# The low halves of seven weight factors: adding DMAs in place of VectorE subtractions

## The chip, the cores and the metric

The kernel runs on one core of a Trainium2 chip. Its time is the device time of one execution in microseconds. Before the change it is 1282.74 us, the median of three runs between 1281.86 and 1282.98.

## What is computed

Two decoder layers over 512 tokens of width 1024, in float32. Each layer projects `x` into three parallel mixers (pooling, retention, sparse attention), projects their concatenation back, adds and normalises, and then runs a gated feed-forward network (FFN) of 2816 columns:

```python
hg = x @ w_gate
hp = jnp.pad(hg, ((0, 0), (CONV_WIDTH - 1, 0), (0, 0)))
hc = conv_b
for kk in range(CONV_WIDTH):
    hc = hc + hp[:, kk:kk + t] * conv_w[kk]
return (jax.nn.gelu(hc) * (x @ w_up)) @ w_down
```

## The kernel before, in words

**Halves.** TensorE works on float32r, a rounded float32. Each float32 operand is therefore split into a high half (the value rounded to float32r) and a low half (what the rounding left), and each product is three matmuls: high by high, high by low, low by high.

**The FFN.** The 2816 columns are 22 groups `f` of 128. In each layer groups 0 to 2 are computed plainly (`ff_plain`). Groups 3 to 21 take gate and up projections together by a scheme of seven block products (`ff_seven`), whose weight operands are called 11, t1, 21, t2, 22, t3 and t4. Each is a tile `w` of 128x2x4x128 numbers (high half and low half, 128x512 each) and is used by one product: 12 matmuls of 256 columns. Between these products stand the matmuls of the down projection (`mm<-w,hT`, 512 columns).

**How a group's weights come about** (`load_seven`). Four DMAs of 256 KB on SyncE's queue fill two tiles `raw`, called b and r here as in the code. VectorE makes two more raw tiles from them by additions: t13 (one addition of 128x1024) and t24 (two of 128x512). From the slices of these four tiles the seven operands are split (`split`): ScalarE writes the high half, and a subtraction writes the low half, on the engine that the table `SEVEN` names (v VectorE, p GpSimd). Groups 20 and 21 of a layer always use VectorE. There are 5 buffers for raw tiles (`NR`) and 14 for w tiles (`NW`); the down projection's weights go through the same buffers, with their low halves by GpSimd (`LO_FFN`). A raw tile's buffer comes free when its last reader is done.

**The order.** All operations are recorded first. A planner (`Plan.schedule`) then gives each engine a fixed order, from a price for each operation (`price`), the latencies between engines, and the number of free buffers; on the chip each engine keeps that order and waits on semaphores. `shares` tells the planner which operations of VectorE and GpSimd it must not place beside each other. A semaphore wait in an engine's or a queue's order holds all that is behind it.

```python
b, r = raw_tile(2, 4, P), raw_tile(2, 4, P)
for out, src in ((b[:, 0], wg[:, 0]), (r[:, 0], wu[:, 0]), (b[:, 1], wu[:, 1]), (r[:, 1], wg[:, 1])):
    nc.sync.dma_start(out, src)
```

Of the kernel before, what the change touches and what calls it, by code (L numbers as in the profile page):

```python
# [10 lines left out]
AF = mybir.ActivationFunctionType  # L11
OP = mybir.AluOpType
AX = mybir.AxisListType
F = mybir.dt.float32
# [11 lines left out]
NFF = FF // P  # L26
# [126 lines left out]
class Plan:  # L153
# [49 lines left out]
    def shares(self, e, m, seen):  # L203

        if e == "vector":
            source = [v for read, v in seen if read and not v.tile.psum and int(np.prod(v.shape[1:])) > 1]
            return len(source) > 1 or (m in ("tensor_scalar", "tensor_copy") and not any(v.tile.psum for _, v in seen))
        return e == "gpsimd" and m != "memset"

    def price(self, op, seen):  # L210
        def size(v):
            return int(np.prod(v.shape[1:]))

        n = max([size(v) for _, v in seen] or [1])
        e, m = op.engine, op.method
        if e == "tensor":
            if m == "transpose":
                return 56 if op.args[2].shape[1] == 64 else 110
            n = size(op.args[2])
            return max(107, n * 0.4537)  # L220
        if e == "scalar":
            extra = sum(isinstance(op.kwargs.get(k), View) for k in ("bias", "scale")) + ("accum_out" in op.kwargs)
            return n * 0.833 + (52 if any(v.tile.psum for _, v in seen) else 95) + 92 * extra
        if e == "vector":
            if m == "reciprocal":
                return 6.3 * n + 70
            scalars = sum(isinstance(a, View) for a in (op.args[2:4] if m == "tensor_scalar" else op.args[2:3]))
            if m in ("tensor_scalar", "tensor_copy") and not any(v.tile.psum for _, v in seen):
                return 0.52 * n + 70 + 58 * scalars
            return 1.04 * n + 70 + 55 * scalars * (m == "scalar_tensor_tensor")  # L230
        if e == "gpsimd":
            if m == "memset":
                return n * 0.9 + 20
            if m == "tensor_copy":
                return n * 3.33 + 120
            if m == "tensor_scalar":
                return n * 1.24 + 120
            if op.args[-1] == OP.pow:
                return n * 165 + 300
            return n * 2.16 + 120  # L240
        byte = n * 4 * max(v.shape[0] for _, v in seen)
        return byte / 330.0

    def schedule(self):
# [35 lines left out]
        def opened(op):  # L280

            out = []
            for t in op.tiles:
                if t.got is None:
                    out.append(t)
                    if t.psum:
                        out += [f for f in t.follow if f.got is None and f not in out]
            return out
# [43 lines left out]
        while left:  # L332
            best = None
            for e in self.ENGINES:
                now = free[e]
                w, r = waiting[e], ready[e]
                while w and w[0][0] <= now:
                    heapq.heappush(r, heapq.heappop(w)[1:])
                cand = None
                skipped = []  # L340
                while r:
                    i = heapq.heappop(r)
                    skipped.append(i)
                    at = placed_at(ops[i[1]])
                    if at is not None and at <= now:
                        cand = (now, *i)
                        break
                    if len(skipped) > LOOK:
                        break
                if cand is None:  # L350

                    opts = []
                    for i in skipped:
                        at = placed_at(ops[i[1]])
                        if at is not None:
                            opts.append((at, *i))
                    for t0, *i in heapq.nsmallest(LOOK, w):
                        at = placed_at(ops[i[1]])
                        if at is not None:
                            opts.append((max(at, t0), *i))  # L360
                    if opts:
                        cand = min(opts)
                for i in skipped:
                    heapq.heappush(r, i)
                if cand is not None and (best is None or cand < best[:3]):
                    best = (*cand, e)
            assert best is not None, "no place for any instruction that is ready"
            start, _, i, e = best
            op = ops[i]
            if (op.rank, i) in ready[e]:  # L370
                ready[e].remove((op.rank, i))
                heapq.heapify(ready[e])
            else:
                waiting[e] = [x for x in waiting[e] if x[2] != i]
                heapq.heapify(waiting[e])
            op.start = start
            end = start + op.cost
            if e == "scalar" and op.method == "activation":
                f = op.args[2]
                if any(f in s for s in FUNCTIONS) and f not in functions:  # L380
                    functions = next(s for s in FUNCTIONS if f in s)
                    end += 1290
            if op.shared:
                held[e == "vector"] = end
            free[e] = end
            if e == "sync":
                free[e] = start + 60
                dma = max(getattr(self, "dma", 0.0), start + 600)
                self.dma = dma + op.cost
                end = self.dma + 1500  # L390
            elif e == "gpsimd":
                free[e] = end + 100
            op.opens = opened(op)
            op.wait = -1
            for t in op.opens:
                place = min(slots[t.key])
                slots[t.key].remove(place)
                t.got, t.after = place[0], place[2]
                if t.psum:
                    used[t.psum] += 1  # L400
            for t in op.tiles:
                t.last, t.by = max(t.last, end), e
                t.left -= 1
                if t.left == 0:
                    slots[t.key].append((t.last + 200, next(number), t))
                    if t.psum:
                        used[t.psum] -= 1
            for u in op.users:
                u.wait -= 1
                u.ready = max(u.ready, end + LATENCY[e][u.engine] * SLACK["wait"])  # L410
                if u.wait == 0:
                    heapq.heappush(waiting[u.engine], (u.ready, u.rank, u.index))
            done.append(op)
            left -= 1
# [12 lines left out]
def trunk(tc, x_d, pos_d, w_in, w_out, w_gate, w_up, w_down, cst_d, prm_d,  # L427
          w1k_d, w1v_d, w2k_d, w2v_d, poolw_d, gn_d, ln1g_d, ln1b_d, ln2g_d, ln2b_d, out_d):
    nc = Plan(tc.nc)
    from contextlib import ExitStack  # L430
    es = ExitStack()
    with es:
# [36 lines left out]
        def engine(who):  # L469
            return nc.gpsimd if who == "p" else nc.vector  # L470
# [46 lines left out]
        def load_seven(l, f):  # L517

            wg, wu = (w[l].rearrange("(h k p) c -> p h k c", p=P, h=2)[:, :, :, f * P:(f + 1) * P] for w in (w_gate, w_up))
# [3 lines that stand above are left out]
            t13, t24 = raw_tile(2, 4, P), raw_tile(2, 4, P)  # L523
            out = {}

            def split(name, src):
                w = w_tile(2, 4, P)
                nc.scalar.copy(w[:, 0], src)
                engine("v" if f >= NFF - 2 else SEVEN[name]).tensor_tensor(w[:, 1], src, w[:, 0].bitcast(F), OP.subtract)
                out[name] = (w[:, 0], w[:, 1])  # L530

            split("11", b[:, 0])
            nc.vector.tensor_tensor(t13, b, r[:, 0:1].to_broadcast([P, 2, 4, P]), OP.add)
            split("t1", t13[:, 0])
            split("21", r[:, 1])
            nc.vector.tensor_tensor(t24[:, 0], t13[:, 0], b[:, 1], OP.add)
            split("t2", t24[:, 0])
            split("22", b[:, 1])
            nc.vector.tensor_tensor(t24[:, 1], t24[:, 0], r[:, 1], OP.add)
            split("t3", t13[:, 1])  # L540
            split("t4", t24[:, 1])
            return out
# [1060 lines left out]

LO_MIX, LO_FFN = "pvv", "p"

SEVEN = {"11": "v", "21": "p", "22": "v", "t1": "v", "t2": "v", "t3": "v", "t4": "v"}

WHO = "vpvp"

# [63 lines left out]
```

## Time and profile before

| what | value |
|---|---|
| median of three runs | 1282.74 us |
| profiled execution, its own time | 1283.03 us |
| span in its profile | 1281.2 us |
| TensorE (PE) busy | 1259.2 us (98%) |
| VectorE (DVE) busy | 1041.5 us (81%) |
| ScalarE (ACT) busy | 707.7 us (55%) |
| GpSimd (POOL) busy | 342.1 us (27%) |
| DMA, mean rate over the span | 96 GB/s |

The span runs from the first to the last instruction; 1.83 us of the profiled execution's own time lie outside it. Busy times are sums of an engine's instructions. A matmul's end is modelled, so the rate of TensorE is read from how many matmuls end in a stretch, not from its busy time. PEld is the loading of weights into TensorE, SPq SyncE's DMA queue.

### The profile page before, as it was taken

How to read it: one execution, taken by the hardware profiler on the slowest of the kernel's cores; microseconds unless marked ns; L12 is line 12 of the kernel's file. 1: busy time of each engine (PE TensorE's matmuls, PEld its weight loads, DVE VectorE, ACT ScalarE, POOL GpSimd, SP SyncE). 2: the span in 40 equal slices, each digit the busy share in tenths (PEclk: the TensorE clock that was granted, in tenths of full speed). 3: DMA queues.
4: the chain of work that ended last, by engine and by line, in shares of the span. 5: the costliest groups of instructions: out<-in, count | busy, mean ns of one | idle time of the engine just before them, and what ended most of it. 6: DMA issues, size and time to landing. Idle time of an engine off the chain costs nothing.

```text
span 1281.2 us, 21536 instructions
## 1 busy us (share of the span) xinstructions
PE 1259.2 (98%) x8044; PEld 1124.9 (88%) x8044; DVE 1041.5 (81%) x1957; ACT 707.7 (55%) x1459; POOL 342.1 (27%) x256
## 2 busy tenths in 40 slices
PE   8999999999999999999999999999999999999996
PEld 6889898879999999999888988888899999999995
DVE  7857896888888988888785788869887989888876
ACT  5445575775655555555333464767565555555540
POOL 1141321424322322212112331233323222222023
PEclk9999999999999999999999999999999999999998
DMA  8422252101343433345342233320023333334321
GB/s 271 120 66 81 87 183 62 34 1 50 93 113 91 128 91 107 109 128 155 121 141 75 67 91 115 124 69 16 2 88 94 92 98 108 117 101 130 98 68 67
DMA packets 142601, 123.24 MB, mean 96 GB/s; under 512 B 6688, under 2 KB 116000, under 8 KB 142496
## 3 DMA queue, kind: packets, MB, share of 16 engines
q1 hardware_dynamic: 142496, 121.86, 31.5%
q8 instruction: 63, 1.03, 0.3%
q14 instruction: 42, 0.34, 0.1%
HBM read 117.65 MB, written 4.19 MB: 95 GB/s over the span
## 4 chain that ended last, share of the span: by engine, by line
PE 93%; DVE 2%; ACT 2%; issue 1%; POOL 1%; DMA 0%; SPq 0%; POOLq 0%; ACTq 0%
PE mm L424 46%; PE s L424 38%; PE tr L424 5%; PE pv L424 4%; ACT P L424 1%; DVE sm L424 1%; DMA x<-in_x 0%; POOL w L424 0%; DVE ps L424 0%; DVE CTl L424 0%; POOL y L424 0%; ACT ot L424 0%; ACT y L424 0%; ACT w L424 0%; DVE w L424 0%
## 5 line engine op out<-in xcount | busy, mean ns | idle before, releaser
L424 POOL TENSOR_TENSOR w<-raw,w 128x1024 fp32r<-128x1024 f32 (+3 forms) x116 | 234.2, 2020 | 663.2 <-ACT w L424 375.0
L424 ACT CAST w<-raw 128x512 fp32r<-128x512 f32 (+2 forms) x403 | 290.9, 742 | 189.1 <-PE s L424 117.8
L424 DVE TENSOR_TENSOR w<-raw,w 128x512 fp32r<-128x512 f32 (+3 forms) x288 | 234.2, 833 | 41.9 <-ACT w L424 36.0
L424 PE MATMUL mm<-w,hT 128*128 128x512 f32 (+1 forms) x1074 | 264.1, 391 | 1.1 <-POOL w L424 1.1
L424 PE MATMUL s<-xq,w 128*128 128x256 f32 x1944 | 250.0, 281 | 0.7 <-ACT xq L424 0.7
L424 PEld LDWEIGHTS s<-xq,w 128*128 128x128 f32 x1944 | 242.6, 189 | 7.1 <-ACT xq L424 1.2
L424 PE MATMUL mm<-w,xT 128*128 128x512 f32 (+3 forms) x1152 | 238.7, 355 | 1.8 <-DVE w L424 1.8
L424 PE MATMUL s<-xs,w 128*128 128x256 f32 x1824 | 234.3, 281 | 0.0
L424 PEld LDWEIGHTS s<-xs,w 128*128 128x128 f32 x1824 | 226.3, 189 | 2.6
L424 PEld LDWEIGHTS mm<-w,hT 128*128 128x128 f32 x1074 | 193.1, 188 | 38.5 <-POOL w L424 1.7
L424 PEld LDWEIGHTS mm<-w,xT 128*128 128x128 f32 x1152 | 191.0, 189 | 26.6 <-ACT xT L424 2.0
L424 DVE TENSOR_TENSOR raw<-raw,raw 128x512 f32<-128x512 f32 (+1 forms) x114 | 106.7, 936 | 5.8 <-DMA raw<-in_w_up 4.3
L424 DVE TENSOR_TENSOR y<-y,mm 128x512 f32<-128x512 f32 (+1 forms) x97 | 63.3, 675 | 22.7 <-PE mm L424 22.3
L424 ACT COPY pq<-s 128x256 f32<-128x256 f32 x152 | 55.3, 368 | 45.5 <-PE s L424 44.9
L424 PE MATMUL mm<-w,mixT 128*128 128x512 f32 x240 | 74.9, 425 | 0.0
L424 POOL TENSOR_TENSOR sm<-sm,mhalf 128x1 f32<-128x1 f32 (+1 forms) x28 | 27.3, 974 | 158.9 <-DVE sm L424 152.2
L424 DVE SCALAR_TENSOR_TENSOR pq<-gu,prm,pq 128x511 f32<-128x511 f32 x76 | 65.8, 865 | 3.1 <-ACT pq L424 2.9
L424 DVE TENSOR_TENSOR PT<-tr,PT 128x384 fp32r<-128x384 f32 (+1 forms) x96 | 49.2, 540 | 9.9 <-ACT PT L424 9.2
L424 ACT ACTIVATE P<-s,sm 128x128 f32<-128x128 f32 (+3 forms) x96 | 49.5, 526 | 13.4 <-DVE sm L424 13.1
L424 ACT CAST PT<-tr 128x384 fp32r<-128x384 f32 (+1 forms) x96 | 41.4, 473 | 23.5 <-PE tr L424 23.1
L424 PEld LDWEIGHTS mm<-w,mixT 128*128 128x128 f32 x240 | 42.2, 189 | 9.9 <-issue 0.2
L424 PE MATMUL mm<-xT,w 128*128 128x512 f32 x192 | 49.6, 400 | 0.0
(195 smaller groups left out, 1676.4 us busy)
## 6 DMA issues: line engine op xcount, KB each, us to landing
raw<-in_w_gate SPq DMA_DIRECT2D x76, 256.0 KB, 3.6
raw<-in_w_up SPq DMA_DIRECT2D x76, 256.0 KB, 4.1
raw<-in_w_down SPq DMA_DIRECT2D x36, 512.0 KB, 4.1
raw<-in_w_in SPq DMA_DIRECT2D x32, 512.0 KB, 4.3
raw<-in_w_out SPq DMA_DIRECT2D x14, 512.0 KB, 3.7
raw<-in_w_in SPq DMA_DIRECT2D x8, 530.0 KB, 4.2
raw<-in_w_down SPq DMA_DIRECT2D x16, 256.0 KB, 2.8
raw<-in_w_in SPq DMA_DIRECT2D x8, 384.0 KB, 3.2
```

Source lines behind the costliest of these rows:

```text
L424: getattr(getattr(self.nc, op.engine), op.method)(*a, **k)
```

## The change

In `split`, the letter d now stands for a third way: ScalarE writes the low half's place with the negative of the value, rounded as the high half is (a copy with scale -1.0), and a DMA issued by GpSimd adds the value to it (`accum_op=OP.add`, from the raw tile to the w tile, 256 KB). All seven operands are set to d, so in groups 3 to 19 of both layers the subtractions are gone. The planner prices the issue at 900 ns on GpSimd, puts the end 4500 ns behind it, and does not count it as sharing with VectorE. The scratch space for GpSimd's DMA descriptors grows from 1024 to 4096 bytes a partition.

```diff
-        return e == "gpsimd" and m != "memset"
+        return e == "gpsimd" and m not in ("memset", "dma_start")
...
         if e == "gpsimd":
+            if m == "dma_start":
+                return 900
...
                 free[e] = end + 100
+                if op.method == "dma_start":
+                    end += 4500
...
                 nc.scalar.copy(w[:, 0], src)
-                engine("v" if f >= NFF - 2 else SEVEN[name]).tensor_tensor(w[:, 1], src, w[:, 0].bitcast(F), OP.subtract)
+                who = "v" if f >= NFF - 2 else SEVEN[name]
+                if who == "d":
+
+                    nc.scalar.activation(w[:, 1], src, AF.Copy, scale=-1.0)
+                    nc.gpsimd.dma_start(w[:, 1], src, accum_op=OP.add)
+                else:
+                    engine(who).tensor_tensor(w[:, 1], src, w[:, 0].bitcast(F), OP.subtract)
...
-SEVEN = {"11": "v", "21": "p", "22": "v", "t1": "v", "t2": "v", "t3": "v", "t4": "v"}
+SEVEN = {"11": "d", "21": "d", "22": "d", "t1": "d", "t2": "d", "t3": "d", "t4": "d"}
...
-    nc = bacc.Bacc("TRN2", target_bir_lowering=False, num_devices=1, dynamic_dma_scratch_size=1024)
+    nc = bacc.Bacc("TRN2", target_bir_lowering=False, num_devices=1, dynamic_dma_scratch_size=4096)
```

## Rows read from the trace of the kernel before

**Rows 1.** The page, part 1: busy time, share of the span, instructions.

```profile
PE 1259.2 (98%) x8044; PEld 1124.9 (88%) x8044; DVE 1041.5 (81%) x1957; ACT 707.7 (55%) x1459; POOL 342.1 (27%) x256
```

**Rows 2.** Stretches of layer one's FFN: length; PE, PEld, DVE, ACT, POOL busy; clock, DMA, GB/s.

```profile
452.99:529.71 76.72, 76.72 (x539) 71.61 (x539) 65.80 (x96) 43.69 (x83) 19.50 (x12) 1.00 0.34 100
529.71:585.92 56.21, 56.21 (x416) 53.34 (x416) 48.88 (x75) 32.85 (x66) 8.76 (x6) 1.00 0.40 120
```

**Rows 3.** Waits of PE, 288 to 660 us: total, times, longest.

```profile
PE mm L424 <- DVE sm L424: 0.6, 1, 0.6
PE mm L424 <- POOL w L424: 0.5, 1, 0.5
```

**Rows 4.** Chain that ended last: start, us, what; two of six like it.

```profile
452.99 7.08 PE s L424 x60
...
529.71 7.07 PE s L424 x60
```

**Rows 5.** ACT by shape, 452.99 to 529.71: busy, mean ns; idle before.

```profile
L424 ACT CAST w<-raw 128x512 fp32r<-128x512 f32 x40 | 24.2, 621 | 23.7 <-PE s L424 19.7 <-PE mm L424 2.2 <-DVE raw L424 0.8
...
L424 ACT ACTIVATE gu<-pq 128x512 f32<-128x512 f32 x5 | 3.2, 632 | 4.3 <-DVE pq L424 4.3
```

**Rows 6.** POOL by shape, 452.99 to 529.71.

```profile
L424 POOL TENSOR_TENSOR w<-raw,w 128x512 fp32r<-128x512 f32 x9 | 12.7, 1411 | 42.4 <-DVE raw L424 14.0 <-PE s L424 12.2 <-PE mm L424 8.9
L424 POOL TENSOR_TENSOR w<-raw,w 128x1024 fp32r<-128x1024 f32 x3 | 7.6, 2548 | 19.4 <-PE s L424 19.4
```

**Rows 7.** Groups by shape, whole span: low halves of 128x512.

```profile
L424 DVE TENSOR_TENSOR w<-raw,w 128x512 fp32r<-128x512 f32 x234 | 166.8, 737 | 27.6 <-ACT w L424 25.4
...
L424 POOL TENSOR_TENSOR w<-raw,w 128x512 fp32r<-128x512 f32 x52 | 74.3, 1429 | 260.4 <-ACT w L424 136.1 <-DVE raw L424 41.5 <-PE mm L424 38.3
```

**Rows 8.** Timeline of SyncE's queue, one group's loads and the next's: start, us.

```profile
472.00 0.37 SPq L424 DMA_DIRECT2D raw<-in_w_gate  x1
472.41 1.05 SPq L424 DMA_DIRECT2D raw<-in_w_up  x2
...
484.14 2.05 SPq L424 DMA_DIRECT2D raw<-in_w_down  x2
487.61 0.37 SPq L424 DMA_DIRECT2D raw<-in_w_gate  x1
```

**Rows 9.** Timeline of DVE, the same group's additions and subtractions.

```profile
478.87 1.21 DVE L424 TENSOR_TENSOR raw<-raw,raw 128x1024 f32<-128x1024 f32 x1
...
480.34 0.68 DVE L424 TENSOR_TENSOR raw<-raw,raw 128x512 f32<-128x512 f32 x1
...
483.91 3.67 DVE L424 TENSOR_TENSOR w<-raw,w 128x512 fp32r<-128x512 f32 x4
488.23 0.69 DVE L424 TENSOR_TENSOR w<-raw,w 128x512 fp32r<-128x512 f32 x1 [0.65 <-ACT w L424]
...
489.61 0.69 DVE L424 TENSOR_TENSOR w<-raw,w 128x512 fp32r<-128x512 f32 x1
```

**Rows 10.** DMA, 452.99 to 529.71: queue's share; issues, KB, us to landing.

```profile
q1 hardware_dynamic: 11808, 7.60, 33.6%
...
raw<-in_w_gate SPq DMA_DIRECT2D x10, 256.0 KB, 3.4
raw<-in_w_up SPq DMA_DIRECT2D x10, 256.0 KB, 4.2
raw<-in_w_down SPq DMA_DIRECT2D x3, 512.0 KB, 4.1
```

**Rows 11.** DMA, whole span: quickest and slowest large ones.

```profile
lnb<-in_ln1b SPq DMA_DIRECT2D x2, 512.0 KB, 6.9
...
out_x<-y SPq DMA_DIRECT2D x2, 256.0 KB, 2.1
```

**Rows 12.** Timeline of DVE, low half of t1 of group 19.

```profile
560.60 0.69 DVE L424 TENSOR_TENSOR w<-raw,w 128x512 fp32r<-128x512 f32 x1
```

**Rows 13.** Timeline of PE, first product with it.

```profile
567.47 1.09 PE L424 MATMUL s<-xs,w 128*128 128x256 f32 x8
```

## The prediction

> **What bounds the kernel now.** I read the page's busy times first: TensorE is busy 98% of 1281.2 us, VectorE 81%, ScalarE 55%, GpSimd 27% [rows 1]. Since a busy TensorE is not one at its peak, I then read stretches of the FFN: over 76.72 us in the middle, five groups of columns, and over 56.21 us near its end TensorE has no idle time at all, at the full clock [rows 2]. Third, TensorE's own waits in the FFN of layer one are 0.6 and 0.5 us, one each [rows 3]; layer two gives the same two figures. Fourth, the chain of waits: bursts of 60 matmuls of 256 columns, 7.08 us each or 118 ns a matmul, come back once a group, six of them from 452.99 to 529.71, so a group takes 76.72/5 = 15.34 us, and TensorE's rate is the same in each [rows 4]. The reader is to see that VectorE, at 86% here (65.80 of 76.72, rows 2), holds TensorE up almost nowhere. What relieving it can give back in both FFNs is 2 x (0.6 + 0.5) = 2.2 us, 0.17%. A measurement of this kernel can tell about 0.2% (2.6 us) from no change. So the question is what the new way costs.
>
> **What goes, and what comes.** Groups 3 to 19 of two layers are 34 groups of seven operands, 238 splits. Gone are 6 x 34 = 204 VectorE subtractions of 0.737 us, 150 us, and 34 on GpSimd of 1.43 us, 49 us [rows 7]. None stands on TensorE's path beyond the 2.2 us above, so I count their going at nothing. Come 238 negations on ScalarE; the nearest rows are the high half itself, 0.621 us, and another function on 128x512, 0.632 us [rows 5]. That is 238 x 0.63 = 150 us. In the five-group stretch it is 35 x 0.63 = 22.1 us on top of 43.69, so ScalarE goes to 65.8 of 76.72, 86%. It is the new busiest engine after TensorE, but it fits. Come also 238 DMA issues on GpSimd, which no row shows. Below, SyncE's issues take about 0.4 us [rows 8]; above, GpSimd's subtraction of the same operand takes 1.43 us. I take 1 us, between the two. In the stretch GpSimd loses five subtractions (7.1 us) of its 19.50 and gains 35 us: 47 of 76.7, 62%. GpSimd is in order, so an issue waits behind a down subtraction of 2.55 us [rows 6] or an earlier issue whose negation is late, and the next down subtraction waits behind it.
>
> **The wait that is longer.** Before, a low half follows its high half by one subtraction. Now it follows by a second ScalarE pass, an issue and a landing. Call L the time from the negation's end to the landing. The trace has no adding DMA and none from buffer to buffer. From below: 256 KB out to memory land in 2.1 us; from above: the slowest large load lands in 6.9 us [rows 11]. The nearest are loads of the same 256 KB, 3.4 and 4.2 us from issue to landing [rows 10]. I take L = 5.0: 4.2, and 0.8 for GpSimd's slower issue and its queue.
>
> The Trainium skill (DMA: Bandwidth & Descriptors, section "Anatomy of one DMA — SWDGE (gpsimd) path") fits a DMA of GpSimd by 2.0 us plus bytes at 436 GB/s, an estimate of 2.6 us for 256 KB. No run here shows it; the loads of that size take 3.4 to 4.2 us. With it L would be about 3.4 and the result would be the first rival.
>
> **Who waits for it: w tiles hardly, raw tiles much.** TensorE uses an operand well after it is ready. In the tightest place that I found, t1 of group 19 is ready at 561.29 and first used at 567.47, 6.2 us later [rows 12, 13]. An extra 0.6 + 5.0 - 0.7 = 4.9 us fits even there. What doesn't stretch is the five raw buffers: their supply is 5 x 15.34 = 76.7 buffer-us a group. One group before: b is loaded from 472.00, and its last subtraction (22, fourth in the row of four) ends at 487.58; at 487.61 the next load starts into it [rows 8, 9]. That is 15.6 us, one period. Loading until the first addition takes 478.87 - 472.00 = 6.9 us; t13 is held from 478.87 to 488.92 and t24 from 480.34 to 490.30, 10 us each.
>
> After, ScalarE's work for a group is 14 passes of 0.62 (8.7 us) and 4.4 us of others ((43.69 - 35 x 0.621)/5), so a pass comes every 8.7/14 x 13.1/8.7 = 0.94 us. Counted from the first addition, with 11 done by then, the negation of 21 ends after 4 passes (3.7), that of 22 after 8 (7.5), t3 after 10 (9.3), t4 after 12 (11.2). Holding times:
> - b: 6.9 + 7.5 + 5.0 = 19.4
> - r: 6.5 + 3.7 + 5.0 = 15.2
> - t13: 9.3 + 5.0 = 14.3
> - t24: 11.2 - 1.5 + 5.0 = 14.7
> - down weights: six raw tiles in five groups (three of 512 KB, three of 256 KB), about 14 us each (4.1 us to land [rows 10], then the high half, TensorE's release of w tiles and GpSimd's turn): 1.2 x 14 = 16.9
>
> Together 80.5 against 76.7. Five buffers then give a group every 80.5/5 = 16.1 us, 0.76 us slower than TensorE needs. Groups 3 and 4 are prepared beside the plain ones; for the other 15 of each layer I count it in full: 30 x 0.76 = 22.8 us. SyncE's queue is in order, so a load that waits for b's buffer holds the down load behind it; that makes the sum rather too small, and the lead of the w tiles makes it rather too large. I leave both out.
>
> The span becomes 1281.2 + 22.8 = 1304.0, with the 1.83 us around it 1305.8; against the median of the runs, 0.3 us under the profiled execution, 1305.5.
>
> The rest is nothing: the mixers' instructions are as before, groups 20 and 21 keep their subtractions, and the larger scratch only takes room. VectorE's additions start sooner as its queue empties, at most the subtraction that is ahead of one, 0.74 us, within the 6.9 us above.
>
> **Rivals.** *The cover holds (no change).* With L = 3.6 each of the four tiles is held 1.4 us less, and the sum is 80.5 - 5.6 = 74.9, under 76.7: TensorE never waits, and the time is 1282.7, or down to 1280.5 if the 2.2 us come back. For it: ScalarE's casts now wait 19.7 us in five groups for TensorE to release w tiles [rows 5], 4 us a group in which raw tiles are held only because the w tiles are full. Against it: at 15.6 us for b the loop takes the whole period already, and ScalarE's passes double.
>
> *The DMA engines fill up.* Loads take 33.6% of them in the stretch for 7.60 MB [rows 10], 3.4 us of all engines per MB or 0.89 us for 256 KB, and 5.2 us a group. Seven additions at the price of a load make 6.2 us more: 11.4 of 15.34, which fits. If one costs double, 12.5 us, the sum is 17.7 us a group, 2.3 too many: 30 x 2.3 = 70 us, 1352. It decides from a price of 1.45 us an addition. The Trainium skill (Collectives: The Full Stack, section "The bandwidth ceiling: the fold count and why AG ≠ RS ≠ AR") says that an adding DMA runs at about half of a copy's rate, since it reads two sources. By that rule the price is double and this rival is the result; no run here shows it yet. For it: an addition has to read the destination too. Against it: a load's price here contains reading device memory in rows of 512 bytes, and the additions stay on the chip in rows of 2 KB.
>
> *ScalarE becomes the bound.* From 529.71 to 585.92 it is busy 32.85 of 56.21 us; with some 20 negations, 12.6 us, it comes to 81%, and bursts of products leave it 1.41 us an operand for two passes and a copy of 0.37 us, 1.6 us. It falls behind by 0.2 us a product, 1.4 us a group, which the down matmuls between give back except in the last few groups: three groups in each layer, 2 x 3 x 1.4 = 8 us, 1291.
>
> *Faster.* VectorE's relief would have to give over 2.6 us. The trace shows 2.2 in the FFNs; more could only come from a better order elsewhere: of the 22.0 us that TensorE is idle in the whole span [rows 1] a sixth, 3.7 us, would make 1279.
>
> **How the numbers follow.** Raw tiles bind 0.50, with a range of its own from 1287 to 1335 (L from 4.0 to 6.9); the cover holds 0.22; DMA engines 0.13; ScalarE 0.10; faster 0.05. The time is that of the likeliest, 1305.5. The range takes in no change, 1280, and reaches to 1356 with the full DMA engines. Slower 0.50 + 0.13 + 0.10 = 0.73, same 0.22, faster 0.05.
>
> **What would show it.** Right: TensorE idle in the FFN, spread over the groups, waiting for the added DMAs; the period between its bursts of 60 near 16.1 us; SyncE's queue waiting for raw buffers that GpSimd's DMAs release; landings near 4 to 5 us; ScalarE near 86% in the middle, VectorE near 60%. Wrong: a period of 15.3 (the cover holds), a DMA share near 100% with landings well over 7 us (DMA engines), or ScalarE without gaps and TensorE waiting for its copies. Should GpSimd's issue take over 1.8 us, GpSimd itself would be the limit (35 x 1.8 + 12.4 = 75 of 76.7), which none of these prices.

## The result: 42 us slower, almost twice the forecast

The kernel with the adding DMAs takes 1324.46 us (four runs, 1320.55 to 1326.26); the kernel before, timed beside it, takes 1282.39. The ratio is 1.0324, between 1.0297 and 1.0351. The forecast was 1305.5, so the sign and the range held, and the size was off by a factor of almost two: +42 us, not +23. The profiled execution took 1326.26 us, with a span of 1324.5.

The page of the kernel after: busy times, DMA queues, and the chain that ended last by engine.

```profile
PE 1273.4 (96%) x8044; PEld 1133.1 (86%) x8044; DVE 896.8 (68%) x1753; ACT 818.5 (62%) x1697; POOL 493.8 (37%) x460
...
q1 hardware_dynamic: 142496, 121.86, 30.2%
q0 software_dynamic: 34272, 62.41, 28.2%
...
PE 74%; DMA 11%; ACT 7%; issue 4%; DVE 3%; POOL 1%; SPq 0%; POOLq 0%; ACTq 0%; DVEq 0%
```

Against [rows 1], TensorE's idle time is 1324.5 - 1273.4 = 51.1 us, where it was 22.0, and its busy time for the same 8044 matmuls is 14.2 us more. Queue q0, GpSimd's adding DMAs, did not exist before: 238 of them take 28.2% of all 16 DMA engines, so 0.282 x 1324.5 / 238 = 1.57 us of the engines each. DMA is now 11% of the chain.

Both FFNs in stretches: length; PE, PEld, DVE, ACT, POOL busy; clock, DMA share, GB/s. First the kernel before, then after; after's last two are neighbours late in layer two.

```profile
330.00:592.00 262.00, 261.45 (x1851) 244.58 (x1849) 226.74 (x325) 146.82 (x282) 63.67 (x35) 1.00 0.36 106
962.00:1222.00 260.00, 259.47 (x1834) 242.57 (x1833) 223.20 (x319) 145.92 (x279) 61.92 (x35) 1.00 0.35 104
```

```profile
330.00:592.00 262.00, 248.83 (x1708) 229.91 (x1708) 141.77 (x200) 185.18 (x367) 131.94 (x127) 0.99 0.98 209
962.00:1222.00 260.00, 244.27 (x1687) 227.10 (x1686) 132.69 (x189) 185.61 (x360) 131.58 (x128) 0.97 0.96 202
1152.00:1184.00 32.00, 32.00 (x228) 29.91 (x227) 17.97 (x26) 23.02 (x47) 16.88 (x17) 1.00 0.94 196
1184.00:1216.00 32.00, 26.75 (x168) 24.51 (x168) 15.85 (x24) 21.98 (x45) 15.84 (x16) 0.89 1.01 211
```

In the same 262 us 1708 matmuls end in place of 1851, so a group's 15.34 us becomes some 15.34 x 1851/1708 = 16.6. The DMA engines' share, which adds up the times of their packets, goes from 36% to 98%. The last two lines show how the loss is spread: 32 us without any idle time, then 32 us with 5 us of it and a granted clock of 0.89.

DMA from 330 to 592 us, after: issues, KB each, median us from issue to landing.

```profile
w<-raw POOLq DMA_DIRECT2D x107, 256.0 KB, 5.8
raw<-in_w_gate SPq DMA_DIRECT2D x33, 256.0 KB, 5.0
raw<-in_w_up SPq DMA_DIRECT2D x33, 256.0 KB, 4.9
raw<-in_w_down SPq DMA_DIRECT2D x10, 512.0 KB, 6.0
```

Not only the adding DMAs are slow to land: the loads, 3.4 to 4.2 us before [rows 10], land in 4.9 to 6.0.

Waits of TensorE over the whole span: total, times, longest.

```profile
PE s L428 <- ACT pq L428: 27.6, 15, 4.5
PE mm L428 <- DVE w L428: 1.8, 1, 1.8
PE s L428 <- DMA w<-raw: 1.6, 1, 1.6
```

TensorE hardly waits for an adding DMA itself. It waits for `pq`, ScalarE's copies of finished products. Why those can be late is seen in the chain of waits near the end of layer two (start us, us, what):

```profile
1182.41 5.84 DMA w<-raw
1188.25 0.02 SPq L428
...
1188.37 7.92 DMA raw<-in_w_gate
...
1196.37 0.07 ACT w L428
...
1197.43 0.87 ACT gu L428 x2
1198.30 0.28 ACT pq L428
...
1198.62 1.44 PE s L428 x10
```

and on ScalarE's and TensorE's timelines (in brackets the idle time before, and what ended it):

```profile
1191.65 0.62 ACT L428 CAST w<-raw 128x512 fp32r<-128x512 f32 x1 [2.33 <-PE s L428]
1192.17 0.37 ACT L428 COPY pq<-s 128x256 f32<-128x256 f32 x1
1196.37 0.62 ACT L428 CAST w<-raw 128x512 fp32r<-128x512 f32 x1 [3.83 <-DMA raw<-in_w_gate]
...
1198.20 0.37 ACT L428 COPY pq<-s 128x256 f32<-128x256 f32 x1
```

```profile
1198.62 1.68 PE L428 MATMUL s<-xs,w 128*128 128x256 f32 x12 [1.19 <-ACT pq L428]
...
1207.91 5.47 PE L428 MATMUL s<-xs,w 128*128 128x256 f32 x24 [4.06 <-ACT pq L428]
```

An adding DMA takes 5.84 us to land. Only then is its raw tile's buffer free, and SyncE's queue issues the next group's load into it. That load takes 7.92 us. ScalarE's next cast in its fixed order needs the load, so ScalarE stands idle for 3.83 us, the copies behind it are late, and TensorE stops for 1.19 us. From 1196.37 us on ScalarE then runs without a gap for over 11 us, and the copy that ends TensorE's longer stop comes only at 1207.50, behind a row of casts and negations:

```profile
1206.97 0.63 ACT L428 ACTIVATE w<-raw 128x512 fp32r<-128x512 f32 x1
1207.50 0.35 ACT L428 COPY pq<-s 128x256 f32<-128x256 f32 x1
```

Six of the passes since 1200.74 are negations, so ScalarE's new work, started late, has a part in the longer stop. The two other stops of over 4 us, up to 554.38 and to 1144.25, also follow casts that waited for loads (3.12 and 2.49 us; 7.32 us). After the stop of 4.06 us, 24 matmuls take 5.47 us, 228 ns each where they took 118 [rows 4]. The stretch of them, in the columns of the stretches above, has a granted clock of 0.50, the lower of the two levels (1.2 GHz):

```profile
1207.90:1213.20 5.30, 5.29 (x25) 5.29 (x26) 2.28 (x3) 2.16 (x5) 1.74 (x2) 0.50 1.10 261
```

### The profile page after: what moved, and what is told of

It is laid out like the page before. It is cut to its first block, busy times and chain, and to the rows that moved or that the text cites. A ratio compares the mean times of both kernels' runs of the same rounds, so it can differ in the third digit from the quotient of the medians.

```text
span 1324.5 us, 22403 instructions
## 1 busy us (share of the span) xinstructions
PE 1273.4 (96%) x8044; PEld 1133.1 (86%) x8044; DVE 896.8 (68%) x1753; ACT 818.5 (62%) x1697; POOL 493.8 (37%) x460
## 3 DMA queue, kind: packets, MB, share of 16 engines
q0 software_dynamic: 34272, 62.41, 28.2%
q8 instruction: 63, 1.03, 0.3%
## 4 chain that ended last, share of the span: by engine, by line
PE 74%; DMA 11%; ACT 7%; issue 4%; DVE 3%; POOL 1%; SPq 0%; POOLq 0%; ACTq 0%; DVEq 0%
PE mm L428 39%; PE s L428 26%; PE tr L428 5%; DMA w<-raw 4%; PE pv L428 4%; ACT w L428 4%; DMA raw<-in_w_gate 3%; DMA raw<-in_w_down 3%; ACT P L428 1%; POOL w L428 1%; DVE raw L428 1%; ACT pq L428 1%; DMA raw<-in_w_up 0%; DMA x<-in_x 0%; DVE sm L428 0%
## 5 line engine op out<-in xcount | busy, mean ns | idle before, releaser
L428 ACT CAST w<-raw 128x512 fp32r<-128x512 f32 (+2 forms) x403 | 294.0, 736 | 159.4 <-PE s L428 47.9
L428 POOL TENSOR_TENSOR w<-raw,w 128x1024 fp32r<-128x1024 f32 (+3 forms) x82 | 180.3, 2200 | 350.9 <-ACT w L428 197.3
L428 POOL DMA_DIRECT2D w<-raw x238 | 207.1, 889 | 202.0 <-ACT w L428 87.9
L428 PE MATMUL s<-xs,w 128*128 128x256 f32 x1824 | 245.8, 287 | 23.9 <-ACT pq L428 22.3
L428 PEld LDWEIGHTS s<-xs,w 128*128 128x128 f32 x1824 | 233.4, 194 | 32.0 <-ACT pq L428 27.5
L428 PE MATMUL s<-xq,w 128*128 128x256 f32 x1944 | 252.9, 282 | 6.1 <-ACT pq L428 5.3
L428 ACT ACTIVATE w<-raw 128x512 fp32r<-128x512 f32 x238 | 149.0, 629 | 0.0
L428 DVE TENSOR_TENSOR raw<-raw,raw 128x512 f32<-128x512 f32 (+1 forms) x114 | 107.0, 938 | 33.9 <-DMA raw<-in_w_up 17.7
L428 DVE TENSOR_TENSOR w<-raw,w 128x1024 fp32r<-128x1024 f32 (+3 forms) x84 | 87.4, 1047 | 13.0 <-ACT w L428 11.3
L428 DVE SCALAR_TENSOR_TENSOR pq<-gu,prm,pq 128x511 f32<-128x511 f32 x76 | 61.0, 802 | 14.6 <-ACT pq L428 14.3
L428 DVE TENSOR_TENSOR pq<-gu 128x512 f32<-128x512 f32 x38 | 29.1, 766 | 43.3 <-ACT gu L428 43.1
L428 ACT ACTIVATE P<-s,sm 128x128 f32<-128x128 f32 (+3 forms) x96 | 49.5, 526 | 13.4 <-DVE sm L428 13.1
```

Source lines behind the costliest of these rows:

```text
L428: getattr(getattr(self.nc, op.engine), op.method)(*a, **k)
```

## The experiments

The expectations name theories by letters: **D**, the DMA engines are full; **H**, raw tiles are held until the landing, and the landing is simply long; **A**, ScalarE's second pass; **O**, the planner's order, made with 4.5 us for the landing. Kernels are changed from the one after, and timed against the kernel before (1282.4 to 1283.1 in each set); ratios are to it.

**1. A copy in place of the addition.** Same bytes, same buffers, same issuing engine.

```diff
-nc.gpsimd.dma_start(w[:, 1], src, accum_op=OP.add)
+nc.gpsimd.dma_start(w[:, 1].bitcast(F), src)
```

> The DMAs of GpSimd copy the value over the low half's place and add nothing (so in groups 3 to 19 the low half is the value itself): same count, same bytes written, same buffers held, same two passes of ScalarE, one source to read instead of two. Theory D (the DMA engines are full): the price of one falls from 1.55 us of all engines to about 0.9, the DMA share in the FFN from 95% to some 75%, and the time returns to 1283 to 1292. Theory H (raw tiles are held too long, whatever the engines' load): landings fall from 5.5 to about 4 us, the holding sum to about 80 of 76.7, and the time is 1300 to 1306. Theory A (ScalarE's doubled passes): 1315 or more.

Measured: 1291.19 us, ratio 1.0064 [1.0049, 1.0079]. Of the 42 us, 33 go. In the traces every engine, and SyncE's queue, has the same order of instructions as in the kernel after, so only the DMAs' own work differs. From its page, its list of DMAs, and its stretches:

```profile
q0 software_dynamic: 19040, 62.41, 13.1%
...
w<-raw POOLq DMA_DIRECT2D x238, 256.0 KB, 3.3
raw<-in_w_gate SPq DMA_DIRECT2D x76, 256.0 KB, 4.2
```

```profile
330.00:592.00 262.00, 258.65 (x1804) 241.27 (x1803) 152.89 (x221) 193.53 (x384) 97.49 (x126) 0.99 0.64 213
```

The same bytes with the same holders cost 0.131 x 1289.7 / 238 = 0.71 us of the engines, 2.2 times less than the addition's 1.57, and land in 3.3 us. That the addition is dearer than a copy makes 33 of the 42 us is thereby shown. It is D's forecast, but H's holding shrinks in the same edit, so the experiment does not part the two alone. Some 9 us over the kernel before remain at a DMA share of 0.64; ScalarE's passes (experiment 3) can be part of them, and the rest is open.

**2. The raw tile let go early.** The DMA adds the high half, from the w tile, in place of the value; no DMA reads the raw tile, so its buffer is free after ScalarE.

```diff
-nc.gpsimd.dma_start(w[:, 1], src, accum_op=OP.add)
+nc.gpsimd.dma_start(w[:, 1], w[:, 0].bitcast(F), accum_op=OP.add)
```

> The adding DMA takes the high half from the w tile as its source and not the value from the raw tile (so the low halves of groups 3 to 19 come out as zero): same count, bytes, adding and ScalarE passes, but a raw tile is free when ScalarE has read it, and no load waits for an added DMA. Theory H: the time returns to 1283 to 1290. Theory D: the DMA engines carry the same, so it stays at 1308 to 1325, with landings of 5 us and more. Theory A: 1315 or more.

Measured: 1383.82 us (1377.82 to 1385.15), ratio 1.0771 [1.0742, 1.0799]. It is slower than the kernel after by 59 us. D and H had forecast less than the kernel after or the same; A's "1315 or more" takes it in, but gives no reason for the 59. Its busy times, DMAs over the whole span, and two links of its chain:

```profile
PE 1297.8 (94%) x8044; PEld 1150.3 (83%) x8044; DVE 889.6 (64%) x1753; ACT 818.5 (59%) x1697; POOL 496.2 (36%) x460
...
w<-w POOLq DMA_DIRECT2D x238, 256.0 KB, 7.3
raw<-in_w_gate SPq DMA_DIRECT2D x76, 256.0 KB, 7.5
raw<-in_w_up SPq DMA_DIRECT2D x76, 256.0 KB, 8.2
```

```profile
440.64 11.98 DMA raw<-in_w_up
...
463.14 9.49 DMA raw<-in_w_up
```

The raw buffers came free sooner, the loads could go out while the adding DMAs of the same group were under way, and both landed later: by the issues and landings in the traces, a load of layer one's FFN has 1.5 additions under way beside it on average in the kernel after, and 2.8 here. The waits for raw buffers had kept part of them apart. So H in its plain form, long landings and nothing else, does not hold: without the holding it should have been faster. The edit is not a clean test of it, though, since the planner, which counts the buffers, puts the engines in another order. Of the 59 us, 24 are longer matmuls (1297.8 us busy in place of 1273.4, at a mean granted clock of 0.968 in place of 0.988) and the others are idle time of TensorE. Why the loads and additions lengthen so much, at a DMA share of only 0.85 and 0.76 in the two FFNs, is not settled.

The same kernel was run once more:

> The kernel whose adding DMAs read the w tile (low halves zero in groups 3 to 19), once more, for one look at whether its time of 1384 comes back and where its loads land. Theory D alone does not price it over 1325; 1375 to 1390 says that the time is the kernel's.

Measured: 1385.74 us in one run. Only the repeat was run; a longer price of the landing in the planner was not tried with this kernel.

**3. ScalarE's part alone.** The negation stays, and VectorE adds where the DMA did. VectorE so takes over GpSimd's 34 subtractions as well.

```diff
-nc.gpsimd.dma_start(w[:, 1], src, accum_op=OP.add)
+nc.vector.tensor_tensor(w[:, 1], src, w[:, 1].bitcast(F), OP.add)
```

> The negation by ScalarE stays, and VectorE adds the value to it in place of the DMA: ScalarE's load of the changed kernel without any added DMA. Theory A: TensorE still waits for ScalarE's copies and the time is 1300 or more. Theories D and H: 1282 to 1287, ScalarE near 86% in the middle of the FFN and nobody late.

Measured: 1286.27 us, ratio 1.0028 [1.0017, 1.0039]. Layer one's stretch:

```profile
330.00:592.00 262.00, 260.96 (x1833) 243.43 (x1834) 219.40 (x335) 195.79 (x389) 41.20 (x20) 1.00 0.36 106
```

The 238 passes on ScalarE and VectorE's added work together cost some 3.6 us, as D and H had it. The passes by themselves are not the cause of the 42.

**4. The negation on VectorE.**

```diff
-nc.scalar.activation(w[:, 1], src, AF.Copy, scale=-1.0)
+nc.vector.tensor_scalar(w[:, 1], src, -1.0, None, OP.mult)
```

> VectorE makes the negation in place of ScalarE, the adding DMAs stay: the DMA load of the changed kernel with ScalarE at its load of before. Theory A: the time falls below 1295. Theories D and H: 1312 to 1330, within about 10 us of the changed kernel, since the landings and the holding of raw tiles are as they were.

Measured: 1340.89 us, ratio 1.0456 [1.0438, 1.0474], 16 us slower than the kernel after, with ScalarE relieved of all that it had gained. GpSimd by shape (busy, mean ns of one; idle before):

```profile
L428 POOL DMA_DIRECT2D w<-raw x238 | 214.1, 1195 | 191.2 <-DVE w L428 151.0 <-PE s L428 18.3 <-issue 7.6
```

GpSimd's issues now wait 151.0 us for VectorE's negations, and one takes 1195 ns on average, where it took 889. So this is A's second miss: a busier ScalarE was the better place. D and H, at 1312 to 1330, are 11 us too low: the edit, meant to leave the DMAs as they were, made their issues later and the engines' order another one.

**5. Four, five and six of the seven by DMA.** The rest by VectorE.

```diff
-SEVEN = {"11": "d", "21": "d", "22": "d", "t1": "d", "t2": "d", "t3": "d", "t4": "d"}
+SEVEN = {"11": "v", "21": "d", "22": "d", "t1": "v", "t2": "v", "t3": "d", "t4": "d"}
```

Five has `t2` as d too, six `t1` as well.

> Four of the seven operands keep the adding DMA, the last reader of each of the four raw tiles: 21 (r), 22 (b), t3 (t13), t4 (t24); 11, t1 and t2 go back to VectorE. Every raw tile is still held until an added DMA has landed, but the DMA engines carry 5.2 + 4 x 1.55 = 11.4 us a group of 15.34 in place of 16.1. Theory D (full DMA engines): 1283 to 1292. Theory H (holding of raw tiles): 1300 to 1320, since the holding times fall only by what the landings fall.

> Five adding DMAs a group (21, 22, t2, t3, t4). Theory D: 5.2 + 5 x 1.55 = 12.95 us of 15.34, 84%: 1282 to 1290. If waiting grows with every added DMA, whatever the sum (theory H): a third of the way from four (1282) to seven (1324), about 1296.

> Six adding DMAs a group (all but 11). Theory D: 14.5 us of 15.34, 95%: little room for bursts, 1286 to 1306, nearer to four than to seven. Theory H: two thirds of the way, about 1310.

Measured: four 1282.42 us, ratio 0.9997 [0.9988, 1.0006]; five 1301.56, 1.0140 [1.0123, 1.0157]; six 1312.03, 1.0229 [1.0214, 1.0244]. Layer one's stretch with four and with five:

```profile
330.00:592.00 262.00, 261.78 (x1849) 244.14 (x1847) 186.19 (x274) 173.45 (x343) 93.74 (x81) 1.00 0.76 173
```

```profile
330.00:592.00 262.00, 256.23 (x1778) 237.13 (x1777) 168.36 (x246) 177.98 (x353) 108.46 (x99) 0.99 0.84 186
```

Four adding DMAs a group cost nothing, and VectorE's relief (226.74 to 186.19 us busy) gives nothing. Waits of SyncE's queue over the whole span (total, times, longest), first with four, then in the kernel after:

```profile
SPq L428 <- DMA w<-raw: 416.2, 94, 13.2
```

```profile
SPq L428 <- DMA w<-raw: 435.0, 94, 12.8
```

The queue waits as long for adding DMAs with four as with seven, and TensorE does not notice. So the wait that the prediction named as the sign of its mechanism does not tell a costly case from a free one. Nor do the loads' landings: by the profile pages, gate and up loads land in 4.7 and 4.5 us with four, at no cost, and in 4.8 and 4.7 with six, at 29 us. What does is TensorE's wait for ScalarE's copies, here with four, five and six (27.6 us with seven):

```profile
PE s L428 <- ACT pq L428: 0.2, 1, 0.2
...
PE s L428 <- ACT pq L428: 12.5, 15, 2.1
...
PE s L428 <- ACT pq L428: 17.2, 16, 2.7
```

D hit with four. With five it missed: 5.2 + 5 x 1.57 = 13.1 us of engine time fits into 15.34, and yet 18 us are lost. With six it missed again (1286 to 1306). The forecast that the waiting grows with each added DMA from four on, about 1296 and 1310, came closer both times, though its own theory, H, missed with four. So with additions a share of 0.84 on average already goes with a loss, well before the engine time of a group is used up. What brings it is not parted by these runs: each step adds engine time, a landing and a ScalarE pass at once.

**6. Engine time without an addition.** One DMA copies the raw tile over both halves of w, 512 KB in place of 256.

```diff
-nc.gpsimd.dma_start(w[:, 1], src, accum_op=OP.add)
+nc.gpsimd.dma_start(w.bitcast(F), src.unsqueeze(1).to_broadcast([P, 2, 4, P]))
```

> The DMAs of GpSimd copy the value over both halves of the w tile and add nothing (512 KB each; in groups 3 to 19 both halves are the value itself). By the copy's measured 0.71 us of all engines for 256 KB, two make 1.42 us, near the 1.55 us of an adding DMA. Theory D: the time is near that of the changed kernel, 1305 to 1325, with a DMA share of 90% or more. If it is not engine time that counts but the adding by itself (its read before the write): 1288 to 1297, as with the single copy.

Measured: 1329.67 us, ratio 1.0364 [1.0346, 1.0383].

```profile
q0 software_dynamic: 34272, 124.80, 26.4%
```

A copy that takes 0.264 x 1325.2 / 238 = 1.47 us of the engines costs 47 us, even more than an addition that takes 1.57. D's forecast is missed by 5 us, but that of the adding by itself (1288 to 1297) by 33. So a DMA need not add to hurt; being this long is enough. The control is not exact: here the high half comes by the DMA too, and the engines' order is another one.

**7. The planner's price and the buffers.** First the landing at 7000 ns, then a sixth raw buffer for one of the w buffers, then both.

```diff
-                    end += 4500
+                    end += 7000
...
-NU, NW, NR = 29, 14, 5
+NU, NW, NR = 29, 13, 6
```

> The changed kernel with the planner's end of an added DMA at 7000 ns and not 4500: only the fixed order of the engines changes. Theory O (the order is built on landings that are too short, and ScalarE's casts stand ahead of TensorE's copies): below 1312. Theory D: 1314 to 1334, since no order makes room on full DMA engines.

> Six raw buffers in place of five, and 13 w buffers in place of 14 (there is no room for both). Theory H: the supply of raw buffers rises by a fifth, to 92 buffer-us a group, and the time falls below 1300. Theory D: 1312 to 1335, and the DMA share in the FFN stays near 95%.

> The changed kernel with the planner's end at 7000 ns, six raw buffers and 13 w buffers together. Theory D: the engines need 16.1 us a group against 15.34, some 23 us over 30 groups, so the time does not fall under 1300 whatever the order and the buffers: 1300 to 1314. Theories O and H together, if they are causes of their own: 12 and 10 us add up and more, below 1300.

Measured: the price alone 1312.59 us, 1.0220 [1.0196, 1.0244]; the buffer alone 1314.22, 1.0249 [1.0229, 1.0269]; both 1302.77, 1.0155 [1.0136, 1.0174]. That is 12, 10 and 22 us less than the kernel after: the two add up. The first lies between the forecasts of O and D, the second is D's (H had below 1300), the third is D's too (O and H had below 1300). With both, the stretches are

```profile
330.00:592.00 262.00, 256.99 (x1801) 238.77 (x1800) 143.69 (x216) 197.07 (x386) 136.53 (x131) 1.00 1.03 218
962.00:1222.00 260.00, 254.92 (x1784) 237.70 (x1783) 141.08 (x204) 195.04 (x379) 137.23 (x132) 0.99 1.01 214
```

20 us over the kernel before remain. Engine time alone seems to give about that: loads 5.2 and seven additions 11.0 make 16.2 us a group, 0.9 over 15.34, and 30 groups make 26 us. But the sum is no floor: by the matmuls that end, a group here takes 15.34 x 1851/1801 = 15.8 us, less than 16.2, and a share of 1.03 shows that packet times overlap. O and H each had a share, 12 and 10 us (H's with a w buffer less, so not by itself). That busy engines make the rest fits these numbers but is argued and not shown. No version here beats the kernel before; the one with four is its equal.

## Why the prediction was right in sign and wrong in size

- **TensorE bounds, and VectorE's relief is worth 2.2 us at most.** Borne out: with four operands moved the time is the same, and no gain above 0.2% showed.
- **The prices on the engines.** A negation took 0.629 us (0.63 forecast). GpSimd's issue took 0.889 us (1 forecast), a plain copy's 0.540. ScalarE is at 185.18 of 262 us, 71%, not 86%. The longer period dilutes it, but experiment 3, which has hardly a longer one, shows only 75% (195.79 of 262). The rest is overlap: on ScalarE's timeline above, an instruction of 0.62 us is followed by the next after 0.52. The negations' own times add up to 150 us, while ScalarE's busy time, which counts an overlap once and is so no plain sum, rose by 818.5 - 707.7 = 110.8. As the price of a pass on the engine, 0.63 us was too much by about a third.
- **Raw tiles bind.** Right as a path: the chain goes from an adding DMA's landing over SyncE's queue and the load to ScalarE, and a sixth raw buffer gives 10 us back. But its sign was the wrong one, a wait of SyncE's queue that is as long with four DMAs, where nothing is lost. And it is not the whole bound: by the prediction's sum six buffers supply 6 x 15.34 = 92.0 buffer-us, enough for no loss at all, and 31 us remained (with one w buffer less).
- **The step that failed: L = 5.0 and 6.9 us for the loads, both sized from a trace with engines a third busy.** The adding DMA costs 1.57 us of the engines, above the 1.45 that the prediction itself gave as the point from which the full engines decide, and far above a load's 0.89. With the engines at 98% it lands 5.8 us after its issue in layer one's FFN (L, from the negation's end, is 5.9 us there on average), and the loads in 4.9 to 5.0. The prediction priced "raw tiles bind" and "DMA engines fill up" as two cases with one chance each. They work together: with dearer DMAs the landings and loads, which the raw tiles wait out, are longer (experiment 1).
- **The sum itself.** With the measured values (four tiles 0.9 us longer, b and r about 1.1 more in loading, 1.2 down tiles about 2) it would be 80.5 + 3.6 + 2.2 + 2.4 = 88.7 buffer-us, 17.7 us a group, where about 16.6 came out. Why less came out is not shown; the w tiles' lead, which I left out, is one candidate. So that the forecast period, 16.1, lies near 16.6 is in part luck: landings taken too short and a sum that asks too much for given landings offset each other.
- **The clock.** Not in the prediction. Of the 43.3 us that the span grew, 29.1 are idle time of TensorE and 14.2 are longer matmuls, with a mean granted clock of 0.988 in place of 0.996. This is an account and not a cause: how much of the 14.2 would have been idle time at full clock is not shown.
- **Rivals.** The cover does hold, but only with four DMAs. ScalarE as the bound: 3.6 us, not 8, with VectorE's added work. The engines' 1352 was too much, since the price is 1.57 and not 1.78; but at 1.57 the same sum gives 26 us, too little. So neither that sum nor the forecast's makes the 42 alone, and the signs of both showed in part: a share near 100%, but landings of 5.8 us and not well over 7.

The rule of the Trainium skill (Collectives: The Full Stack, "The bandwidth ceiling: the fold count and why AG ≠ RS ≠ AR"), stated there for the adding DMAs of a reduce-scatter between cores, is that an adding DMA reads two sources and so runs at about half of a copy's rate. Experiment 1 agrees on one core: 1.57 against 0.71 us, 2.2 times. The fit of the Trainium skill for GpSimd's DMAs (DMA: Bandwidth & Descriptors, "Anatomy of one DMA — SWDGE (gpsimd) path") gives an estimate of 2.6 us for 256 KB. The copies beside this kernel's loads come near it, with 3.3 us of which the issue itself takes 0.540; the additions, with 5.5 us and an issue of 0.889, do not.

## What to carry to other kernels

Before work is moved to DMAs, add up the DMA engines' time per period as if they were one more engine, with an addition at twice a copy, and stay well below the period: here 76% was free and 84% cost 1.4%. The share alone does not give the cost: seven copies at 64% cost 0.6%, and seven additions cost 3.2% at 98%, but only 1.6% at 103% with another order and one more raw buffer. Landing times read from a trace with idle engines don't hold once the engines are busy, and everything that is held until a landing (raw tiles, then loads, then an in-order engine behind the loads) grows with them. When a wait is the expected sign of a cost, ask whether a version without the cost would show it too.

## What was not expected of the hardware

- An addition from one on-chip buffer to another costs 1.57 us of all 16 DMA engines for 256 KB, more than the 0.89 us of a load of that size from device memory [rows 10], and its issue on GpSimd takes 0.889 us against a copy's 0.540.
- Letting buffers go earlier made the kernel 59 us slower; more loads and additions were under way together, and they landed in 7.3 to 8.2 us.
- GpSimd's issue slowed from 889 to 1195 ns when VectorE made the negations.
- A stop of TensorE can cost more than its own time: after 4.06 us of waiting the granted clock was 0.50, and 24 matmuls ran at 228 ns each in place of 118.
- ScalarE's passes of 0.63 us overlap: 238 more of them raised its busy time by 0.47 us each.
